# Layer 0 of a decoder trunk: six projection units on h without shift, and a completion of h in place

## The chip, the core and the metric

One core of a Trainium2 chip runs the whole program in one launch. The metric is device time in microseconds (us) of one execution. Before the change the median of three runs is 1299.08 us (1296.54 to 1302.62).

The engines: PE (matmuls), ACT (activations), DVE (vector operations), POOL (a second, slower vector engine), and SP, which issues most of the DMAs. Each works through its own queue in order and waits on semaphores of the others.

## The reference, cut to what matters

Two layers, 512 tokens, 1024 channels, float32. Each layer computes:

```python
def mixer_layer(x, c, positions, w_ada, b_ada, g_norm, w_in, ...):
    mod = jax.nn.silu(c) @ w_ada + b_ada                # (1, 3 * 1024)
    shift, scale, gate = jnp.split(mod, 3, axis=-1)
    h = rms_norm(x, g_norm) * (1.0 + scale[:, None, :]) + shift[:, None, :]
    z = h @ w_in                                         # (1, 512, N_IN)
    (fq, fk, fv, ff, fg, dq, dckv, diq, dik, diw, dg,
     sq, sk, sv, sg, merge) = jnp.split(z, points, axis=-1)
    ...                                                  # three causal mixers: y_fox, y_dsa, y_sb
    m_fox, m_dsa, m_sb = jnp.split(jax.nn.sigmoid(merge), 3, axis=-1)
    mixed = m_fox * (y_fox @ w_br_fox) + m_dsa * (y_dsa @ w_br_dsa) + m_sb * (y_sb @ w_br_sb)
    return x + gate[:, None, :] * (mixed @ w_out)
```

`c` is one vector, so `shift`, `scale` and `gate` are one number per channel, and each of the three is a product of a vector of 1024 with a matrix of 1024x1024 (4 MB of `w_ada`). Since h = n * s + shift (n the normed x, s = g_norm * (1 + scale)), a projection is h @ W = (n * s) @ W + shift @ W, and shift @ W is one number for each column of W.

## The kernel before

**Products.** h is kept channel-major in `hH`, `hL`: eight chunks `k` of 128 channels (partitions) by 512 tokens. Each float32 operand is split into a high part of reduced precision and the remainder, and each product is three matmuls (high*high, high*low, low*high; `mm3`). A weight tile is loaded into `raw` (or `qst`), its high part `wh` is made on ACT (L117), its low part `wl` on DVE (L121). A *unit* is 128 columns of `w_in` against all eight chunks: 24 matmuls of 512 columns into one PSUM bank.

**Order.** PE and SP work in the order of the code. The main stream is a generator; beside it a planner runs threads (attention heads, spills, later conditioning) by a clock of its own that counts PE time. ACT, DVE and POOL are ordered by a scheduler; a part of the first layer's opening puts DVE in the order of the code. `self.t(shape, type, tag, n)` takes the next of `n` buffers of a tag: a tile waits until the one that had the buffer before has been read. The DMA semaphores are eight in number, so that a ninth transfer waits for the first.

**The opening of layer 0 before.** `load_x` brings x, `setup` the parameters, `first_x` (L365) transposes x on PE and takes the norm's factors, `rope_tables` (L239) makes the tables of sines. `opening_first` (L872) then goes through four blocks `b` of 256 channels. For each, `ada_first` (L311) loads eight tiles of `w_ada` (256 columns of shift and of scale), and the sums are made on DVE (`ada_sum`) and, in part, as one-column matmuls on PE (`ada_mm`, L329); `ada_close` adds them. `scale_h` (L413) and `rest_h` (L420) then make `hH` and `hL` of the block's two chunks, and `step` runs products with them: the *small* columns (208 matmul columns wide, two banks), and three units, fox q, fox k and a fox gate. All eight chunks of x are written back to memory by `spill` (L395). Behind the opening the stream goes on with `diq(0)` (matmuls of 256 columns), the values, and the units of the merge gates (`gate0(m)`, L1045; columns from `O_MERGE`), of which `gate0(0)` comes after the second tile of values and `gate0(1)`, `gate0(2)` with the next pair.

## Time and profile before

| | us |
|---|---|
| median of three runs | 1299.08 (1296.54 to 1302.62) |
| the profiled execution: its own time | 1301.89 |
| its span | 1300.2 |
| mean granted clock of TensorE in it | 0.992 |
| PE busy | 1258.1 (97%) |
| DVE busy | 973.1 (75%) |
| ACT busy | 720.1 (55%) |
| first product / first matmul of `diq(0)` | 25.46 / 70.60 |

The profile is of one execution. A busy time is the time in which an engine had an instruction in work; matmuls overlap, so that their pace is read from their start times and not from the length of one. "Granted clock" is the share of full speed that TensorE was allowed. A bracket behind a timeline's row says how long the engine was idle just before and what ended it.

### The profile page before, as it was taken

What the parts mean: (1) busy time and instruction counts of PE and PEld (TensorE: products, weight loads), DVE (VectorE), ACT (ScalarE), POOL (GpSimd) and SP (SyncE); (2) the same over time, 40 slices, a digit from 0 to 9 for tenths busy, and PEclk for the clock granted to TensorE, in tenths of its full rate; (3) what the DMA queues carried; (4) which work ended last, traced back from release to release, by engine and by line L of the source; (5) the groups of instructions that cost most, each with busy time, mean ns of one, the idle gap of its engine ahead of it and who ended that gap; (6) DMA issues with size and microseconds to landing.
All of it is one profiled execution on the core that took longest, in us unless ns stands there. A gap on an engine that the chain in (4) does not pass through costs nothing.

```text
span 1300.2 us, 19627 instructions
## 1 busy us (share of the span) xinstructions
PE 1258.1 (97%) x7057; PEld 1087.3 (84%) x7057; DVE 973.1 (75%) x2059; ACT 720.1 (55%) x1415; POOL 154.0 (12%) x343
## 2 busy tenths in 40 slices
...
GB/s 285 151 163 99 82 113 113 99 88 75 114 91 89 115 88 90 113 137 94 148 122 91 106 66 97 81 67 99 81 65 98 66 98 66 98 81 106 94 100 73
DMA packets 193458, 133.33 MB, mean 103 GB/s; under 512 B 9457, under 2 KB 188225, under 8 KB 193361
## 3 DMA queue, kind: packets, MB, share of 16 engines
...
HBM read 125.74 MB, written 6.29 MB: 102 GB/s over the span
## 4 chain that ended last, share of the span: by engine, by line
PE 74%; DVE 14%; DMA 5%; issue 3%; ACT 2%; SPq 0%; POOL 0%; DVEq 0%; POOLq 0%; ACTq 0%
PE pg L65 57%; PE pt L65 8%; PE pa L65 5%; PE pt L69 4%; DMA raw<-in_w_in_dram 3%; DVE wl L121 3%; DVE fm L667 2%; DVE pr L668 1%; DVE score L614 1%; DVE ada L280 1%; DVE m L613 1%; ACT wh L117 1%; DVE pt L121 1%; DVE qst L123 1%; DMA vs<-in_x_dram 1%
## 5 line engine op out<-in xcount | busy, mean ns | idle before, releaser
L65 PE MATMUL pg<-hH,wh 128*128 128x512 f32 (+1 forms) x848 | 340.4, 401 | 0.5 <-ACT wh L117 0.5
L65 PE MATMUL pg<-hH,wl 128*128 128x512 f32 (+1 forms) x848 | 332.9, 393 | 0.8 <-DVE wl L121 0.8
L65 PE MATMUL pg<-hL,wh 128*128 128x512 f32 (+1 forms) x848 | 333.0, 393 | 0.0
L121 DVE TENSOR_TENSOR wl<-raw,wh 128x1024 fp32r<-128x1024 f32 (+1 forms) x178 | 217.8, 1224 | 89.6 <-ACT wh L117 88.9
L117 ACT ACTIVATE wh<-raw 128x1024 fp32r<-128x1024 f32 (+1 forms) x178 | 187.7, 1054 | 159.6 <-PE pg L65 79.3
L65 PEld LDWEIGHTS pg<-hH,wl 128*128 128x128 f32 x848 | 160.2, 189 | 37.7 <-DVE wl L121 1.0
L65 PEld LDWEIGHTS pg<-hL,wh 128*128 128x128 f32 x848 | 161.5, 190 | 26.6
L65 PEld LDWEIGHTS pg<-hH,wh 128*128 128x128 f32 x848 | 161.1, 190 | 26.8 <-ACT wh L117 0.7
L65 PE MATMUL pg<-wh,hH 128*128 128x256 f32 x448 | 128.7, 287 | 0.0
L65 PE MATMUL pg<-wh,hL 128*128 128x256 f32 x448 | 126.5, 282 | 0.0
L65 PE MATMUL pg<-wl,hH 128*128 128x256 f32 x448 | 125.8, 281 | 0.0
L117 ACT ACTIVATE pt<-pt 128x512 fp32r<-128x512 f32 x192 | 83.3, 434 | 74.9 <-PE pt L69 73.2
L65 PE MATMUL pg<-y,wh 128*128 128x512 f32 x384 | 121.2, 396 | 0.0
L121 DVE TENSOR_TENSOR pt<-pt,pt 128x512 fp32r<-128x512 f32 x192 | 92.9, 484 | 25.9 <-ACT pt L117 23.6
L624 ACT ACTIVATE pr<-pr,nm 128x128 f32<-128x128 f32 (+3 forms) x128 | 71.6, 560 | 67.5 <-DVE nm L623 67.0
L69 PE MATMUL pt<-ident,pr 128*128 128x128 f32 x480 | 85.9, 275 | 3.0 <-DVE pr L668 2.7
L626 ACT ACTIVATE pr<-pr,den 128x128 f32<-128x128 f32 (+3 forms) x128 | 71.1, 559 | 27.0 <-DVE den L625 26.2
L65 PEld LDWEIGHTS pg<-wh,hH 128*128 128x128 f32 x448 | 84.8, 189 | 0.7
L65 PEld LDWEIGHTS pg<-wl,hH 128*128 128x128 f32 x448 | 84.7, 189 | 0.7
L65 PEld LDWEIGHTS pg<-wh,hL 128*128 128x128 f32 x448 | 84.4, 188 | 0.0
L65 PE MATMUL pa<-pt,vs 128*128 128x512 f32 (+3 forms) x256 | 71.3, 352 | 11.6 <-DVE pt L121 10.9
L65 PEld LDWEIGHTS pg<-y,wh 128*128 128x128 f32 x384 | 70.2, 188 | 14.0
(216 smaller groups left out, 2337.4 us busy)
## 6 DMA issues: line engine op xcount, KB each, us to landing
raw<-in_w_in_dram SPq DMA_DIRECT2D x134, 512.0 KB, 3.8
raw<-in_w_ada_dram SPq DMA_DIRECT2D x32, 512.0 KB, 3.5
raw<-in_w_out_dram SPq DMA_DIRECT2D x16, 512.0 KB, 3.7
y<-in_w_ada_dram SPq DMA_DIRECT2D x24, 256.0 KB, 5.4
raw<-in_w_br_fox_dram SPq DMA_DIRECT2D x8, 512.0 KB, 3.7
raw<-in_w_br_sb_dram SPq DMA_DIRECT2D x8, 512.0 KB, 4.1
raw<-in_w_br_dsa_dram SPq DMA_DIRECT2D x8, 512.0 KB, 4.6
yf<-xd ACTq DMA_DIRECT2D x16, 256.0 KB, 2.9
```

What stands on the lines that cost most here:

```text
L65: self.nc.tensor.matmul(o, s, m, start=first, stop=last, skip_group_check=True)
L69: self.nc.tensor.transpose(o, i, self.ident[:n, :n])
L117: self.nc.scalar.activation(out, in_, AF.Copy, scale=scale)
L121: self.nc.vector.tensor_tensor(out, in_, hi.bitcast(F32), ALU.subtract)
L123: self.nc.vector.scalar_tensor_tensor(out, in_, scale, hi.bitcast(F32), ALU.mult, ALU.subtract)
L280: nc.vector.scalar_tensor_tensor(acc, v[:, j, :], self.sc[:, k:k + 1], acc, ALU.mult, ALU.add)
L613: self.pin(nc.vector.max(m8, s))
L614: nc.vector.match_replace(s, m8, s, SENT)
L624: nc.scalar.activation(p, p, AF.Exp, bias=nm, scale=-1.0, accum_out=den)
L626: nc.scalar.activation(p, p, AF.Copy, scale=den)
L667: nc.vector.tensor_tensor_scan(rev, rev, rev, 1.0, ALU.mult, ALU.bypass)
L668: nc.vector.tensor_tensor(s[:, :n - 1], s[:, :n - 1], u[:, 1:n], ALU.mult)
```

## The change

The first layer's opening is written anew as `first_layer`, with DVE in the order of the code throughout it.

- The parameters are loaded on ACT's queue, ahead of x; `c` gets its transposition first (`condition`), the rest follows (`params`).
- x is transposed at once, seven chunks into seven banks and the eighth after them, and n = x * rstd is made for each chunk (`norm`).
- Only *scale* is loaded in four quarters of 256 channels, with the columns of six units: fox q, k and gate (units 0 to 2) and the merge gates 0 to 2 (units 4, 5 and 3). `scale_sum` adds a quarter (quarter 0 on PE alone, with 16 one-column matmuls; the others on DVE, with a part on PE). `chunks(b)` makes `hH` and `hL` of n * s, without shift, splits the weights, and then puts n * s in the place of n.
- All six units run on this h, quarter by quarter.
- *Shift* is loaded meanwhile, in two halves of eight tiles of 128x512. `shift_sum` adds a half: ACT scales three tiles, POOL adds these, DVE adds five. `shift_close` takes the sum across partitions with eight one-column matmuls. `complete(k)` makes `hH` and `hL` anew in place, with shift.
- `unit_shift` multiplies the unsplit weights of the six units with shift: 48 one-column matmuls into one bank, from which a bias for each unit is taken. It enters the three gates through their Tanh, and units 0 to 2 by an Identity in place.
- The tables of rope, and a part of the spill, come behind the last quarter's `chunks`. The small columns come at the end, on the completed h, both halves after all else. `gate0` returns at once for the three gates that are done.

```diff
+    def first_layer(self, fox, posts, mod):
+        nc, xt = self.nc, self.xt
...
+        gates = O_MERGE
+        singles = (fox[0], fox[1], fox[2], gates + 256)
+        homes = (("qst", 6), ("kh", 5), ("kl", 5), ("yf", 4))
...
+        def load_scale(b):
+            scale[b] = []
+            for j in range(4):
+                v = self.t([P, 2, 256], F32, *(("pt", 4) if b == 2 else ("y", 8)))
+                src = w_ada[j * 256:(j + 1) * 256, D + b * 256:D + b * 256 + 256]
+                nc.sync.dma_start(v, src.rearrange("(k p) n -> p k n", p=P))
+                scale[b].append(v)
...
+        def load_shift(i):
+            shift[i] = []
+            for k in range(KC):
+                v = self.t([P, 512], F32, *(("pt", 4) if i == 0 and k >= 4 else ("y", 8)))
+                nc.sync.dma_start(v, w_ada[k * P:(k + 1) * P, i * 512:(i + 1) * 512])
+                shift[i].append(v)
...
+        def load_chunks(b):
+            if b % 2 == 0:
+                load_single(0, b // 2)
+            load_scale(b)
+            if b % 2 == 0:
+                load_single(1, b // 2)
+            load_gates(b)
+            if b % 2 == 0:
+                load_single(2, b // 2)
+                load_single(3, b // 2)
+        load_chunks(0)
+        load_chunks(1)
...
+        norm = lambda k: nc.vector.tensor_tensor(xn[k], xc[k], rb, ALU.mult)
+        norm(0)
+        norm(1)
+        def scale_sum(b, pe):
...
+            ops = [(scale[b][j][:, i, :], self.sc[:, 2 * j + i:2 * j + i + 1]) for j in pe for i in range(2)]
+            ops += [(acc, self.ones)] if js else []
+            for n, (v, s) in enumerate(ops):
+                for c in range(2):
+                    self.mm(pt[:, c:c + 1], v[:, c * P:(c + 1) * P], s, n + c == 0, n + 1 == len(ops))
+            c = slice(2 * b, 2 * b + 2)
+            nc.vector.tensor_tensor(mod[1][:, c], pt[:, 0:2], self.prm[:, 32 + 2 * b:34 + 2 * b], ALU.add)
+            nc.vector.scalar_tensor_tensor(mod[1][:, c], mod[1][:, c], 1.0, self.prm[:, 8 + 2 * b:10 + 2 * b], ALU.add, ALU.mult)
...
+        def chunks(b):
             ks = (2 * b, 2 * b + 1)
...
+            for k in ks:
+                nc.scalar.activation(self.hH[:, k, :], xn[k], AF.Copy, scale=mod[1][:, k:k + 1])
+            if b % 2 == 0:
+                split_single(0, b)
+            for k in ks:
+                nc.vector.scalar_tensor_tensor(self.hL[:, k, :], xn[k], mod[1][:, k:k + 1],
+                                               self.hH[:, k, :].bitcast(F32), ALU.mult, ALU.subtract)
+            if b % 2 == 0:
+                split_single(1, b)
+            split_gates(b)
+            if b % 2 == 0:
+                split_single(2, b)
+                split_single(3, b)
+            for k in ks:
+                nc.scalar.activation(xn[k], xn[k], AF.Copy, scale=mod[1][:, k:k + 1])
+        pss = {u: self.ps("g") for u in range(3)}
+        order = (0, 1, 4, 5, 2, 3)
+        def unit(u, b):
...
+            for k in (2 * b, 2 * b + 1):
+                if u < 4:
+                    w = [x[:, k, :] for x in wt[u]]
+                else:
+                    w = [x[:, k - 2 * b, (u - 4) * P:(u - 3) * P] for x in gw[b]]
+                self.mm3(ps, *w, h[0][k], h[1][k], k == 0, k == KC - 1)
...
+        def shift_sum(i):
+            v = shift[i]
+            for k in (1, 4, 7):
+                nc.scalar.activation(v[k], v[k], AF.Copy, scale=self.sc[:, k:k + 1])
+            nc.gpsimd.tensor_tensor(v[1], v[1], v[4], ALU.add)
+            nc.gpsimd.tensor_tensor(v[1], v[1], v[7], ALU.add)
+            acc = self.t([P, 512], F32, "tmp", 2)
+            for k in (0, 2, 3, 5, 6):
+                if k == 0:
+                    nc.vector.tensor_scalar(acc, v[k], self.sc[:, k:k + 1], None, ALU.mult)
+                else:
+                    nc.vector.scalar_tensor_tensor(acc, v[k], self.sc[:, k:k + 1], acc, ALU.mult, ALU.add)
+            sums[i] = [acc, v[1]]
+        def shift_close(i):
+            if i == 0:
+                self.late_ps = self.ps("a")
+            pt = self.late_ps
+            for n, acc in enumerate(sums[i]):
+                for j in range(4):
+                    self.mm(pt[:, 4 * i + j:4 * i + j + 1], acc[:, j * P:(j + 1) * P], self.ones, i + n + j == 0, n == 1)
+            c = slice(4 * i, 4 * i + 4)
+            nc.vector.tensor_tensor(mod[0][:, c], pt[:, c], self.prm[:, 24 + 4 * i:28 + 4 * i], ALU.add)
+        def complete(k):
+            nc.scalar.activation(self.hH[:, k, :], xn[k], AF.Identity, bias=mod[0][:, k:k + 1])
+            nc.vector.scalar_tensor_tensor(self.hL[:, k, :], xn[k], mod[0][:, k:k + 1],
+                                           self.hH[:, k, :].bitcast(F32), ALU.add, ALU.subtract)
+        def unit_shift(ks):
+            for k in ks:
+                for u in range(6):
+                    if u < 4:
+                        w = raws[u, k // 4][:, k % 4, :]
+                    else:
+                        w = raws["g", k // 2][:, k % 2, (u - 4) * P:(u - 3) * P]
+                    self.mm(self.late_ps[:, 8 + u:9 + u], w, mod[0][:, k:k + 1], False, k == KC - 1)
+        load_chunks(2)
+        scale_sum(0, range(4))
+        chunks(0)
+        norm(2)
+        norm(3)
+        load_chunks(3)
+        self.load_positions()
+        self.forget_bias()
+        for b in range(4):
+            for u in order[:4]:
+                unit(u, b)
             if b < 3:
...
+                scale_sum(b + 1, (3,))
+                chunks(b + 1)
+                if b == 0:
+                    for k in range(4, KC):
+                        norm(k)
+                if b == 1:
+                    load_shift(0)
+                if b == 2:
+                    self.rope_tables()
+                    shift_sum(0)
+                    load_shift(1)
+                    for k in range(3):
+                        nc.sync.dma_start(self.xd[k], xc[k])
+                    small = [self.small_raw(0, j) for j in range(2)]
             else:
...
+                shift_close(0)
+                for k in range(4):
+                    complete(k)
+                unit_shift(range(4))
+            for u in order[4:]:
+                unit(u, b)
+        shift_sum(1)
+        shift_close(1)
+        for k in range(4, KC):
+            complete(k)
+        unit_shift(range(4, KC))
+        ws = [self.split(v) for v in small]
+        bias = self.t([P, 16], F32, "bias")
+        nc.vector.tensor_copy(bias[:, 0:6], self.late_ps[:, 8:14])
+        nc.vector.tensor_scalar(bias[:, 8:14], bias[:, 0:6], 0.5, None, ALU.mult)
+        for m, u in enumerate((4, 5, 3)):
+            self.mix[m] = self.t([P, S], F32, "mix", 8)
+            nc.scalar.activation(self.mix[m], pss[u], AF.Tanh, scale=0.5, bias=bias[:, 8 + u:9 + u])
+        for u in range(3):
+            nc.scalar.activation(pss[u], pss[u], AF.Identity, bias=bias[:, u:u + 1])
+            posts[u](pss[u])
...
+        return xc, ws
...
-            self.new_h()
-            h = self.h()
-            rb = self.rows(st["r"], "t", range(NB))
-            yield from self.opening_first(xc, rb, mod, fox, h, sps, sms, post)
-            pss = [None, None, self.gate_ps]
-            self.spawn(self.small_post(l, sms), 3.0)
-            self.spawn(self.spill(xc), 10.0)
...
+            for u in range(2):
+                for kc in range(KC):
+                    yield from self.gemm_b(sps[u], ws, NSM, (2 * u, 2 * u + 1), (kc,))
+                self.small_take(sms, sps[u])
+            self.spawn(self.small_post(l, sms), 2.0)
+            self.spawn(self.spill(xc[3:], 3), 1.0)
+            self.mark(("fox", l, "pair", 0), 0.0)
+            return
...
         def gate0(m):
+            if self.mix[m]:
+                return
             self.mix[m] = self.t([P, S], F32, "mix", 8)
...
-        xc, r, self.rest_x = self.first_x(xt)
-        self.forget_bias()
-        self.rope_tables()
-        carry = {"r": r}
+        xc, carry = None, {}
...
+            self.load_params()
             self.xt = self.load_x()
             self.setup()
             self.go(self.program(out))
```

Where the instructions stand, at three places.

DVE, between the last quarter's work and the end of the opening. Before, the tables of rope (`rt`, `ropeC`, `ropeS`) stand among the sums of the first block (`fm`), ahead of the first `hL`:

```order
L280 SCALAR_TENSOR_TENSOR fm_235<-y_248,sc_129,fm_235 128x256
L268 SCALAR_TENSOR_TENSOR rt_45_213<-rt_44_212,rt_45_213 128x128
L280 SCALAR_TENSOR_TENSOR fm_235<-y_248,sc_129,fm_235 128x256
L269 TENSOR_SCALAR rt_45_213<-rt_45_213 128x128
L280 SCALAR_TENSOR_TENSOR fm_235<-y_254,sc_129,fm_235 128x256
L270 TENSOR_SCALAR rt_45_213<-rt_45_213 128x128
L280 SCALAR_TENSOR_TENSOR fm_235<-y_254,sc_129,fm_235 128x256
L272 TENSOR_SCALAR ropeS_198<-ropeS_198 128x4x32
L346 TENSOR_TENSOR mod_9_90<-pa_232,prm_125 128x2
L349 SCALAR_TENSOR_TENSOR mod_9_90<-mod_9_90,prm_125 128x2
L346 TENSOR_TENSOR mod_8_89<-pa_232,prm_125 128x2
```

After, they stand between the last quarter's `hL` (above these rows) and the sum of shift's first half (`tmp_567`; `y_423` and so on are its tiles); `mod_9_90` is shift, `wl_743` the low part of the small columns' first weights:

```order
L268 TENSOR_SCALAR rt_118_552<-rt_118_552 128x128
L270 TENSOR_SCALAR ropeS_537<-ropeS_537 128x4x32
L970 TENSOR_SCALAR tmp_567<-y_423,sc_154 128x512
L972 SCALAR_TENSOR_TENSOR tmp_567<-y_427,sc_154,tmp_567 128x512
L972 SCALAR_TENSOR_TENSOR tmp_567<-y_429,sc_154,tmp_567 128x512
L972 SCALAR_TENSOR_TENSOR tmp_567<-pt_433,sc_154,tmp_567 128x512
L972 SCALAR_TENSOR_TENSOR tmp_567<-pt_435,sc_154,tmp_567 128x512
L983 TENSOR_TENSOR mod_9_90<-pa_636,prm_150 128x4
L987 SCALAR_TENSOR_TENSOR hL_215<-vs_216,mod_9_90,hH_214 128x512 x4
L970 TENSOR_SCALAR tmp_695<-y_573,sc_154 128x512
L972 SCALAR_TENSOR_TENSOR tmp_695<-y_577,sc_154,tmp_695 128x512
L972 SCALAR_TENSOR_TENSOR tmp_695<-y_579,sc_154,tmp_695 128x512
```

The tables went from the front of the opening to a place ahead of the sum of shift.

ACT, at the end of the opening. Before, the last two `hH`, then copies of the small columns' result and the high parts of `diq(0)`'s weights (`wh_706`, `wh_712`):

```order
L418 ACTIVATE hH_225<-tm_607,mod_8_89 128x512
L418 ACTIVATE hH_225<-tm_610,mod_8_89 128x512
L469 COPY tm_648<-pt_223 128x416
L485 ACTIVATE rt_148_759,ssq_758<-tm_648 128x128
L485 ACTIVATE rt_149_761,ssq_758<-tm_648 128x128
L469 COPY tm_662<-pt_224 128x416
L117 ACTIVATE wh_706<-raw_704 128x1024
L485 ACTIVATE rt_150_763,ssq_758<-tm_662 128x128
L117 ACTIVATE wh_712<-raw_710 128x1024
```

After, the last tile of shift's second half is scaled (`y_587`), then come the first half's four `hH`, the second half's, the high parts of `diq(0)`'s weights (`wh_889`, `wh_895`), the Identity passes on the banks of units 0 to 2 (`pg_220` to `pg_222`), and a table load, right behind which the three gates' Tanh stand (`mix_753` from the bank `pt_308` first):

```order
L964 ACTIVATE y_587<-y_587,sc_154 128x512
L986 ACTIVATE hH_214<-vs_216,mod_9_90 128x512 x4
L117 ACTIVATE wh_742<-raw_592 128x832
L117 ACTIVATE wh_746<-raw_596 128x832
L986 ACTIVATE hH_214<-vs_217,mod_9_90 128x512 x4
L117 ACTIVATE wh_889<-raw_887 128x1024
L117 ACTIVATE wh_895<-raw_893 128x1024
L117 ACTIVATE pr_163_927<-y_925 128x128
L1045 ACTIVATE pg_220<-pg_220,bias_750 128x512
L1045 ACTIVATE pg_221<-pg_221,bias_750 128x512
L1045 ACTIVATE pg_222<-pg_222,bias_750 128x512
L1043 ACT_TABLE_LOAD
```

The four `hH` of the first half stand behind the scaling of the second half's last tile, and the Tanh of the gates behind the next projection's weights.

PE, at the end of the opening. Before, the last chunks of the three units (`pg_314`, `pg_326`, `pg_337`) are followed by `diq(0)` (`pt_716`):

```order
L65 MATMUL pg_337<-hH_225,wl_328 128x512
L65 MATMUL pg_337<-hH_225,wh_327 128x512
L65 MATMUL pg_337<-hL_226,wh_327 128x512
L65 MATMUL pg_337<-hH_225,wl_328 128x512
L65 MATMUL pt_716<-wh_706,hH_225 128x256
L65 MATMUL pt_716<-wl_707,hH_225 128x256
```

After, the weights' products with shift (`pa_636`) are followed by the small columns (`pt_785`); their second half, 48 rows on, goes to `pt_786`, which takes the bank of `pt_308`, the first merge gate's:

```order
L65 MATMUL pa_636<-mod_9_90,qst_288 128x1 x2
L65 MATMUL pa_636<-mod_9_90,qst_223 128x1
L65 MATMUL pa_636<-mod_9_90,kh_233 128x1
L65 MATMUL pa_636<-mod_9_90,kl_237 128x1
L65 MATMUL pa_636<-mod_9_90,yf_239 128x1
L65 MATMUL pa_636<-mod_9_90,qst_288 128x1 x2
L65 MATMUL pt_785<-wh_742,hH_214 128x208
L65 MATMUL pt_785<-wl_743,hH_214 128x208
L65 MATMUL pt_785<-wh_742,hL_215 128x208
```

What stood among the units' products before, the small columns, now stands alone between the completion and `diq(0)`.

## Rows read from the trace of the kernel before

**Rows 1.** The page's head: the span, and each engine's busy time, its share of the span and its instructions.

```profile
span 1300.2 us, 19627 instructions
...
PE 1258.1 (97%) x7057; PEld 1087.3 (84%) x7057; DVE 973.1 (75%) x2059; ACT 720.1 (55%) x1415; POOL 154.0 (12%) x343
```

**Rows 2.** The timeline of PE in 0 to 71 us: start, length of one, engine, line, operation, out<-in, tile (weights, then result), how many in a row; in brackets the idle time before and what ended it.

```profile
14.26 6.82 PE L65 MATMUL pa<-sc,y 128*128 128x1 f32 x32
...
25.46 0.54 PE L65 MATMUL pt<-wh,hH 128*128 128x208 f32 x1 [1.72 <-ACT hH L418]
...
31.93 0.41 PE L65 MATMUL pt<-wl,hH 128*128 128x208 f32 x1
32.14 0.38 PE L65 MATMUL pt<-wh,hL 128*128 128x208 f32 x1
...
40.45 3.41 PE L65 MATMUL pa<-sc,y 128*128 128x1 f32 x16
...
50.88 0.27 PE L65 MATMUL pt<-wl,hH 128*128 128x208 f32 x1
50.99 0.28 PE L65 MATMUL pt<-wh,hL 128*128 128x208 f32 x1
...
54.20 1.84 PE L65 MATMUL pa<-sc,pt 128*128 128x1 f32 x16
...
69.67 0.40 PE L65 MATMUL pg<-hH,wl 128*128 128x512 f32 x1
...
70.60 0.28 PE L65 MATMUL pt<-wh,hH 128*128 128x256 f32 x1
```

**Rows 3.** Windows of 10 us: length, then busy time (and instructions) of PE, PEld, DVE, ACT and POOL, the clock granted to PE, DMA share, GB/s.

```profile
40.00:50.00 10.00, 10.00 (x41) 9.11 (x39) 6.80 (x15) 1.38 (x2) 0.00 (x0) 0.53 0.69 223
...
80.00:90.00 10.00, 8.15 (x68) 7.65 (x67) 7.10 (x15) 5.48 (x8) 0.00 (x0) 1.00 0.76 207
90.00:100.00 10.00, 8.28 (x68) 7.88 (x66) 6.55 (x14) 7.23 (x15) 1.74 (x5) 1.00 0.20 69
100.00:110.00 10.00, 9.04 (x71) 8.88 (x72) 9.77 (x24) 7.75 (x17) 3.10 (x6) 1.00 0.36 108
110.00:120.00 10.00, 9.75 (x78) 9.34 (x77) 9.90 (x24) 7.42 (x16) 2.33 (x5) 1.00 0.54 155
```

**Rows 4.** The waits behind the opening, 80 to 102 us, as rows of three timelines: four of PE, one of ACT, one of DVE.

```profile
85.30 0.44 PE L69 MATMUL pt<-ident,rq 128*128 128x128 f32 x2 [0.17 <-DVE rq L439]
...
89.55 0.41 PE L69 MATMUL pt<-ident,rq 128*128 128x128 f32 x2 [1.68 <-DVE rq L439]
...
96.39 0.39 PE L65 MATMUL pt<-y,qst 128*128 128x256 f32 x1 [0.96 <-DVE y L121]
...
100.96 0.66 PE L69 MATMUL pt<-ident,tmp 128*128 128x128 f32 x4 [1.71 <-DVE tmp L439]
...
85.49 1.06 ACT L117 ACTIVATE wh<-raw 128x1024 fp32r<-128x1024 f32 x1 [2.63 <-DMA raw<-in_w_in_dram]
...
86.58 1.23 DVE L121 TENSOR_TENSOR wl<-raw,wh 128x1024 fp32r<-128x1024 f32 x1 [1.34 <-ACT wh L117]
```

**Rows 5.** Instructions of 0 to 70 us by line, engine, operation and shape: busy time in us, mean ns of one; then the idle time before them and what ended it.

```profile
L422 DVE SCALAR_TENSOR_TENSOR hL<-tm,mod,hH 128x512 fp32r<-128x512 f32 x8 | 5.8, 747 | 0.9 <-ACT hH L418 0.7
...
L418 ACT ACTIVATE hH<-tm,mod 128x512 fp32r<-128x512 f32 x8 | 5.5, 720 | 15.7 <-DVE tm L417 15.7
...
L121 DVE TENSOR_TENSOR wl<-raw,wh 128x1024 fp32r<-128x1024 f32 x3 | 3.7, 1224 | 0.8 <-ACT wh L117 0.8
L117 ACT ACTIVATE wh<-raw 128x1024 fp32r<-128x1024 f32 x3 | 3.2, 1055 | 0.6 <-DMA raw<-in_w_in_dram 0.6
L379 ACT COPY mix<-pt 128x512 f32<-128x512 f32 x5 | 2.8, 574 | 1.1 <-PE pt L69 1.1
...
L117 ACT ACTIVATE wh<-qst 128x512 fp32r<-128x512 f32 x4 | 2.5, 620 | 0.2 <-DMA qst<-in_w_in_dram 0.2
...
L121 DVE TENSOR_TENSOR wl<-raw,wh 128x832 fp32r<-128x832 f32 x2 | 2.0, 1020 | 0.3 <-ACT wh L117 0.3
...
L271 ACT ACT_TABLE_LOAD x1 | 1.3, 1283 | 0.0
...
L268 DVE SCALAR_TENSOR_TENSOR rt<-rt,rt 128x128 f32<-128x128 f32 x2 | 0.6, 286 | 0.0
...
L264 DVE TENSOR_SCALAR rt<-rq 128x128 f32<-128x128 f32 x2 | 0.4, 222 | 0.0
...
L271 ACT ACTIVATE ropeC<-rt 128x128 f32<-128x128 f32 x1 | 0.3, 309 | 0.2 <-DVE rt L270 0.2
L209 POOL TENSOR_SCALAR_AFFINE_SELECT pen<-pen 128x128 f32<-128x128 f32 x1 | 0.3, 297 | 0.0
```

**Rows 6.** DMA: what was moved in each of 40 slices of 0 to 60 us (1.5 us each), the total of that stretch, and from the whole page the KB of an issue and the median us from issue to landing.

```profile
GB/s 0 115 421 423 418 52 160 288 272 282 332 309 264 279 288 307 338 341 356 354 346 346 184 302 242 285 323 288 350 367 315 56 0 0 11 0 12 238 192 0
DMA packets 17605, 14.19 MB, mean 236 GB/s; under 512 B 3441, under 2 KB 17089, under 8 KB 17601
...
raw<-in_w_in_dram SPq DMA_DIRECT2D x134, 512.0 KB, 3.8
...
yf<-xd ACTq DMA_DIRECT2D x16, 256.0 KB, 2.9
```

256 lines of the change are left out of this document (93 added, 163 removed).

## The prediction

> **What bounds the kernel now.** I read the page's totals first: PE is busy 97% of the span [rows 1], so time can only come from the stretches where PE waits, or from work that it no longer does. The windows say where the first layer's opening has such stretches. PE starts its first product only at 25.46, having waited 1.72 us for ACT's hH [rows 2]; it then works without a gap to the end of the opening at 70.60, but partly at the lower of its two clock levels: the granted clock is 0.53 in 40 to 50 [rows 3], and the 208-column products start 0.21 us apart at 31.93 against 0.11 at 50.88 [rows 2]. The next idle PE stands behind the opening: 8.15 and 8.28 busy in 80 to 100, and there the weights are what is late (ACT waited 2.63 for one to land, DVE 1.34 for ACT) [rows 3, 4]. From 100 on DVE has become the full engine: 9.77 and 9.90 of 10 [rows 3].
>
> **What the change does, step by step.** It starts products earlier (only `scale` is needed for the first h) and pulls three gate units forward; it pays with a second pass over h, with one-column products for the weights' shift, and with a chain at the end that nothing covers.
>
> *Start.* The transposes of the first half of x are done by 14.26 [rows 2], as before. Then come 16 one-column products for quarter 0 of scale: 16 such took 1.84 [rows 2], so 16.1. Add a short DVE step (estimate 0.3) and one hH, 0.72 [rows 5]: products start at about 17.3 instead of 25.46, 8.2 earlier.
>
> *Quarters.* A quarter is 6 units of 2 chunks of 3 products, 36 x 0.2325 (four products from 69.67 to 70.60, [rows 2]) = 8.4, plus 0.7 for the six one-column products of the next scale (6 x 0.115). I take the first 6.7 us at the lower clock, as from 25.46 to 32.14 before [rows 2]; this costs 3.3. The four leading units of quarters 0 to 3 then end at about 26, 35, 44.5 and 54. Loads should not bound it: columns of six units are 1.5 MB more than of three, on the 14.19 MB of the first 60 us, and from 12 to 45 us most slices moved 260 to 370 GB/s, with little left to move behind 47 [rows 6].
>
> *The tail.* At 54 PE wants the sum of the first half of shift. It stands on DVE behind hL of quarter 3 (I have it end at 49.9) and behind the tables of rope, which before stood among the sums of the first block. Their price: two tables of four scalar steps (0.22), three of 0.28, one sine (0.31) and one more scalar step (0.22) [rows 5], 2 x 2.26 = 4.5, and an estimated 1.1 for the start and the hand-overs between ACT and DVE: 55.5. The first step of the sum ends at 56.1 and the other four (0.75 each, hL's price [rows 5]) at 59.1: PE waits 5. From the first step hangs a chain of buffers, because a tile of the second half of shift can only be loaded into the place that this step frees:
>
> transfer of y 2.9 (such a tile's time in [rows 6]) to 59.0; scaling on ACT 0.65 (between 0.62 and 0.72 [rows 5]) to 59.7; an add on POOL; the last tile's transfer, 2.9, which waits for that add; its scaling. No POOL add of 512 columns is in the trace: POOL took 0.30 for a select over 128 columns [rows 5], so four times that is 1.2; the bounds are 0.3 and 2.4 (twice), and I take 1.2. The last tile is scaled at 64.4. Only behind it, in ACT's order, stand the four hH of the first half (4 x 0.72 = 2.9, 67.3), and the hL follow (the last 0.75 later, 68.0); behind these on DVE the five steps of the second sum (3.5, 71.5), eight one-column products (1.7 at the lower clock's 0.213, from 3.41 for 16 [rows 2]; 0.9 at the higher), the bias (0.2), hH x 4 (2.9), the last hL (0.75), and the low part of the small weights, 1.02 [rows 5]: **78.1**. PE's own work beside it (two units, 48 one-column products) fits in the 19 us from 59.1.
>
> Then small: two halves of 48 products at 0.11 [rows 2]. The first runs at once, to 83.4. The second wants the bank that Tanh of the first gate unit frees. On ACT this Tanh stands behind two splits of the next unit's weights. Their loads wait for the small split on DVE: 78.1 + 3.8 [rows 6] + 1.06 [rows 5] = 82.9, the second split at 84.0, three Identity passes over 512 columns (0.57 each, the price of the copies from PSUM [rows 5]) after DVE has made the bias at 85.2, 86.9; a table load 1.28 [rows 5], Tanh 0.6 as such a copy: 88.8. The second half ends at 94.1, and there the next projection (128x256, at 70.60 before [rows 2]) begins.
>
> *The opening's sum.* Before, that projection begins at 70.60, with three gate units still to come later: 72 x 0.232 = 16.7, so 87.3 on the same count. After: 94.1. **Loss 6.8.** PE's sum alone would be 17.3 + 4 x 8.4 + 2.1 + 3.3 + 10.6 for small + 9 for the one-column work of the tail = 76; 18 us of the tail are waiting.
>
> *Given back.* The waits behind the opening (0.17, 1.68, 0.96 and 1.71, together 4.5 [rows 4]) come from weights that landed late. After the change these are split by 84 to 85, 9 us ahead of their use. Bounds 0 (the releaser by name is the rotation on DVE, and may stay) and 4.5; I take 3.2, since ACT's 2.63 and DVE's 1.34 of waiting there [rows 4] stand right ahead of the two larger ones.
>
> *Taken away.* The three gate units no longer fill the stretch 100 to 120, where DVE is full: 16.7 us of PE work leave, with only 3 x 1.22 of DVE work [rows 5]. PE is still 9.04 and 9.75 busy there [rows 3], and attention is paced by PE's clock in the planner, so other projections move up. Bounds 0 and 6.5 (half of 16.7 - 3.7); I take 1, near the idle time that the stretch shows now.
>
> Rests: 37 more PE instructions, the ACT and DVE passes of the completion: all inside the tail already counted. Spills and the small loads now stand behind the last shift tile on SP's queue, and land by 69, before they are wanted: nothing.
>
> **Sum.** 6.8 - 3.2 + 1.0 = +4.6 on the profiled execution's 1301.89, 1306.5. That execution was 2.8 above the median of the runs, 1299.08; on the median's scale 1303.7, +0.35%.
>
> **The rivals.** *A, slower: the filler is missed.* Nothing is given back and DVE's stretch costs 4 to 6 more, because units with posts on DVE take the gates' place: 6.8 + 4 = +11, 1310. For it: 9.77 and 9.90 [rows 3]. Against: PE's waits [rows 4] lie ahead of that stretch and begin with weights. It decides if DVE's projections in 90 to 130 stand without slack.
>
> *B, faster: the tail is hidden.* If the rope tables or the buffers cost PE little (hand-overs quicker, POOL at 0.3, the Tanh earlier), the opening ends near PE's sum plus some 6 us of waiting, 82: 5 ahead of 87.3, and with 3 given back -8: 1291. For it: the start is 8 earlier and no product is lost. Against: four steps of the chain are transfers and ACT passes whose prices the trace shows [rows 5, 6].
>
> *C, slower: the tail at the lower clock.* From 59 to 78 PE does almost nothing but one-column products and waiting. Behind such work the trace shows a granted clock of 0.53 in 40 to 50 and 0.213 per one-column product [rows 2, 3]; yet in 80 to 100, with 1.8 us idle of 10, it stayed at 1.00 [rows 3]. The first half of small at the lower clock would hide (78.1 + 10.2 = 88.3, before Tanh at 88.8); if the second also runs so, 48 x 0.10 = 4.9 more: 1308.6. The Trainium skill ("TensorE: Matmul & The Clock Gate", section "Part 1: The HAM clock gate") says that "the default state is throttled, and activity releases the throttle". By that rule this tail, with its waits, ends throttled, and the sum would be C's; the row of 40 to 50 agrees, those of 80 to 100 show waits without a fall, and none shows a tail of this length.
>
> *D, the change doesn't start early.* If quarter 1 or 2 waits for its weights (eight transfers in flight, shared with scale), the 8 us of the start go: 6 to 8 slower than the forecast, 1310.
>
> **How the numbers follow.** Forecast 0.44, A 0.22, B 0.16, C 0.12, D 0.06. About 0.5% (6.5 us) is what a measurement of this kernel can tell from no change, so the borders are 1292.6 and 1305.6. The forecast's own range, 1300 to 1307, lies within them but for 0.08 of its 0.44; of B 0.13 is below, 0.03 within; of A 0.06 within, 0.16 above; of C 0.02 within, 0.10 above; D above. Faster 0.13, same 0.47, slower 0.40. The range 1292 to 1313 leaves out most of B and the far end of A.
>
> **What would show it.** Right: first product near 17; PE idle or one-column from 54 to 78; the wait for y's transfer and Tanh as releasers there; the 128x256 projection at 94; smaller waits at the same place in the program behind. Wrong: that projection before 88 (B), or after 97 (C, D); or a like opening and a longer 100 to 140 with DVE as releaser (A).

## The result

| | before | after |
|---|---|---|
| median of the runs, us | 1298.67 (1296.54 to 1302.62) | 1316.51 (1316.05 to 1317.95) |
| ratio | | 1.0136 (95% interval 1.0110 to 1.0161) |
| profiled execution: time, span | 1301.89, 1300.2 | 1316.05, 1314.3 |
| first product / first 256-column product of `diq(0)` | 25.46 / 70.60 | 18.63 / 106.05 |

The median of the kernel before is over four executions now, and so differs from the 1299.08 given at the start. The changed kernel is 17.8 us slower by the medians (14.1 by the two profiled executions); 4.6 were forecast, and the range ended at 1313. The head of its page (against [rows 1]):

```profile
span 1314.3 us, 19829 instructions
...
PE 1265.5 (96%) x7134; PEld 1104.0 (84%) x7134; DVE 975.7 (74%) x2061; ACT 734.2 (56%) x1443; POOL 158.6 (12%) x347
```

Its PE timeline in the opening (against [rows 2]):

```profile
12.88 4.55 PE L65 MATMUL pa<-sc,y 128*128 128x1 f32 x32
18.63 0.80 PE L65 MATMUL pg<-hH,wh 128*128 128x512 f32 x1 [1.20 <-ACT hH L929]
...
57.67 0.39 PE L65 MATMUL pt<-hH,pr 128*128 128x512 f32 x1
62.41 1.16 PE L65 MATMUL pa<-ones,tmp 128*128 128x1 f32 x8 [4.35 <-DVE tmp L972]
63.43 1.85 PE L65 MATMUL pa<-ones,y 128*128 128x1 f32 x8
65.53 0.59 PE L65 MATMUL pa<-mod,qst 128*128 128x1 f32 x2 [0.25 <-DVE mod L983]
65.98 0.56 PE L65 MATMUL pa<-mod,kh 128*128 128x1 f32 x2
66.41 0.57 PE L65 MATMUL pa<-mod,kl 128*128 128x1 f32 x2
66.83 1.42 PE L65 MATMUL pa<-mod,yf 128*128 128x1 f32 x6
...
74.52 1.42 PE L65 MATMUL pa<-mod,yf 128*128 128x1 f32 x6
75.80 0.77 PE L65 MATMUL pg<-hH,wh 128*128 128x512 f32 x1
...
80.69 0.95 PE L65 MATMUL pa<-ones,tmp 128*128 128x1 f32 x8
...
82.78 0.38 PE L65 MATMUL pa<-mod,qst 128*128 128x1 f32 x2 [0.26 <-DVE mod L983]
...
91.45 0.99 PE L65 MATMUL pa<-mod,qst 128*128 128x1 f32 x4
92.30 0.52 PE L65 MATMUL pt<-wh,hH 128*128 128x208 f32 x1
...
100.60 0.36 PE L65 MATMUL pt<-wh,hH 128*128 128x208 f32 x1 [0.34 <-ACT mix L1043]
...
106.05 0.29 PE L65 MATMUL pt<-wh,hH 128*128 128x256 f32 x1
```

Read the counts: a `shift_close` of eight one-column products stands as two rows of x8, that is 16 PE instructions, and one chunk's six products with shift as 12. **Each float32 one-column product is two PE instructions.** From 65.53 to 75.80 PE does the first 24 of them, from 82.78 to 92.30 the second 24, 0.20 to 0.21 us per instruction. From 62.41 until the small columns begin at 92.30 PE has no wait longer than 0.26. The forecast's wait for DVE ahead of that is there (4.35 at 62.41, forecast 5). The windows of the same stretch (columns as in [rows 3]) show the clock that went with it:

```profile
60.00:70.00 10.00, 7.34 (x37) 7.28 (x38) 3.38 (x5) 3.11 (x5) 2.54 (x2) 0.66 0.71 220
70.00:80.00 10.00, 10.00 (x38) 9.13 (x39) 5.62 (x9) 2.58 (x4) 0.00 (x0) 0.50 0.24 50
80.00:90.00 10.00, 9.74 (x57) 9.47 (x56) 4.77 (x7) 2.56 (x4) 0.00 (x0) 0.67 0.17 52
90.00:100.00 10.00, 10.00 (x60) 10.00 (x60) 2.80 (x5) 5.56 (x8) 0.00 (x0) 0.64 0.86 249
```

0.50, the lower level, in all of 70 to 80, and 0.64 to 0.67 around it. ACT's timeline shows the chain of Tanh that the forecast had found: two transfers, two splits, Identity, a table load.

```profile
67.61 0.72 ACT L964 ACTIVATE y<-y,sc 128x512 f32<-128x512 f32 x1 [4.62 <-DMA y<-in_w_ada_dram]
...
82.76 2.56 ACT L986 ACTIVATE hH<-vs,mod 128x512 fp32r<-128x512 f32 x4 [8.77 <-DVE mod L983]
90.69 1.06 ACT L117 ACTIVATE wh<-raw 128x1024 fp32r<-128x1024 f32 x1 [5.36 <-DMA raw<-in_w_in_dram]
94.30 1.06 ACT L117 ACTIVATE wh<-raw 128x1024 fp32r<-128x1024 f32 x1 [2.56 <-DMA raw<-in_w_in_dram]
...
98.56 1.28 ACT L1043 ACT_TABLE_LOAD   x1
```

Tanh follows at 99.86 and releases the second half of the small columns at 100.60; PE waited for it only 0.34, since it came late itself. The chain hangs on the close of shift's second half: the row at 82.76 waits for its `mod`, and that close stands on PE behind the first 24 products.

Behind the opening the forecast gain is there. PE busy in the 100 us from the 256-column projection on, after:

```profile
106.05:206.05 100.00, 98.75 (x655) 90.42 (x654) 83.34 (x189) 69.19 (x142) 22.03 (x39) 1.00 0.33 96
```

and before, in the same place of the program (the waits of [rows 4] among them):

```profile
70.60:170.60 100.00, 95.22 (x629) 86.53 (x628) 82.01 (x184) 69.23 (x133) 19.83 (x37) 1.00 0.42 122
```

4.78 us idle before, 1.25 after. Much of the rest of the span's gain behind the projection is not waits but the pace of the products; "The pitch" below is on that.

### The profile page after: what moved, and what is told of

Same layout as the page of the kernel before. It is cut to its first block, busy times and chain, and to the rows that moved or that the text cites. A ratio compares the mean times of both kernels' runs of the same rounds, so it can differ in the third digit from the quotient of the medians.

```text
span 1314.3 us, 19829 instructions
## 1 busy us (share of the span) xinstructions
PE 1265.5 (96%) x7134; PEld 1104.0 (84%) x7134; DVE 975.7 (74%) x2061; ACT 734.2 (56%) x1443; POOL 158.6 (12%) x347
## 4 chain that ended last, share of the span: by engine, by line
PE 60%; DVE 20%; DMA 9%; ACT 5%; issue 4%; POOL 0%; ACTq 0%; DVEq 0%; SPq 0%; POOLq 0%
PE pg L65 46%; PE pt L65 8%; DMA raw<-in_w_in_dram 5%; DVE wl L121 4%; PE pa L65 4%; PE pt L69 3%; ACT wh L117 2%; DVE fm L595 2%; DVE ada L278 2%; DVE m L541 1%; DVE pt L121 1%; DVE score L542 1%; DVE pr L596 1%; DMA yf<-in_w_in_dram 1%; DVE qst L123 1%
## 5 line engine op out<-in xcount | busy, mean ns | idle before, releaser
L65 PE MATMUL pg<-hH,wh 128*128 128x512 f32 (+1 forms) x824 | 329.4, 400 | 2.3 <-ACT hH L929 1.2
L65 PE MATMUL pg<-hH,wl 128*128 128x512 f32 (+1 forms) x824 | 321.3, 390 | 0.8 <-DVE wl L121 0.8
L65 PE MATMUL pg<-hL,wh 128*128 128x512 f32 (+1 forms) x824 | 321.0, 390 | 0.0
L121 DVE TENSOR_TENSOR wl<-raw,wh 128x1024 fp32r<-128x1024 f32 (+1 forms) x174 | 212.4, 1222 | 101.7 <-ACT wh L117 100.9
L117 ACT ACTIVATE wh<-raw 128x1024 fp32r<-128x1024 f32 (+1 forms) x174 | 183.4, 1054 | 156.5 <-PE pg L65 81.4
L65 PEld LDWEIGHTS pg<-hH,wl 128*128 128x128 f32 x824 | 156.4, 190 | 34.5 <-DVE wl L121 1.0
L65 PEld LDWEIGHTS pg<-hH,wh 128*128 128x128 f32 x824 | 156.9, 190 | 26.7 <-ACT wh L117 1.3
L65 PEld LDWEIGHTS pg<-hL,wh 128*128 128x128 f32 x824 | 157.0, 191 | 25.2 <-DVE hL L933 0.9
L552 ACT ACTIVATE pr<-pr,nm 128x128 f32<-128x128 f32 (+3 forms) x128 | 71.5, 558 | 61.8 <-DVE nm L551 61.0
```

Of the source, the lines that this page charges most:

```text
L65: self.nc.tensor.matmul(o, s, m, start=first, stop=last, skip_group_check=True)
L117: self.nc.scalar.activation(out, in_, AF.Copy, scale=scale)
L121: self.nc.vector.tensor_tensor(out, in_, hi.bitcast(F32), ALU.subtract)
L552: nc.scalar.activation(p, p, AF.Exp, bias=nm, scale=-1.0, accum_out=den)
```

## The experiments

Theory 1: PE's own one-column products bind the tail. Theory 2, the prediction's: the chain of buffers, scaling, POOL and transfers does. Theory 3: the lower clock is the loss. Theory 4: the three gates were worth keeping as filler. Theories 5 to 7 are on the pitch, at the end (5: the places of the tiles in SBUF set it; 6: the chip or the day; 7: the place of `wh`, by itself in 7a, against the others in 7b). Where no diff names another base, the base is the changed kernel. "Projection" is the first 256-column product.

**e1, a quarter of the products with shift.**

```diff
-            for k in ks:
+            for k in ks[:1]:
                 for u in range(6):
```

> This kernel leaves out 36 of the 48 one-column products of the weights with shift (chunks 0 and 4 alone are done), so the bias of the six units is incomplete. Theory 1 (these products, two PE instructions each, 96 in all at 0.214 us, are what the tail waits for): the second sum on DVE, ready at 75.8 before, takes over, the 256-column projection starts at 96 to 98 instead of 106.05, and the time falls by 8 to 10, to about 1307. Theory 2 (the chain of buffers, ACT scaling, POOL add and transfers sets the end of the tail, as the prediction had it): 0 to 2 less, 1314 to 1316.

1308.48, ratio 1.0062 (1.0046 to 1.0079): 8.0 less than the changed kernel. 36 of the 48 products are left out. Its PE timeline:

```profile
75.77 1.76 PE L65 MATMUL pa<-ones,tmp 128*128 128x1 f32 x8 [2.20 <-DVE tmp L972]
...
79.50 0.59 PE L65 MATMUL pa<-mod,qst 128*128 128x1 f32 x2 [0.25 <-DVE mod L983]
...
82.08 0.52 PE L65 MATMUL pt<-wh,hH 128*128 128x208 f32 x1
...
97.32 0.29 PE L65 MATMUL pt<-wh,hH 128*128 128x256 f32 x1
```

The small columns begin at 82.08, 10.2 sooner: the products were the path to them. Now PE does wait for the second sum (2.20 at 75.77): the forecast's chain is the next thing behind, and not the first. The projection starts at 97.32, 8.7 sooner and inside theory 1's 96 to 98, but that number has a second cause. The scheduler gave ACT another order here, with Tanh ahead of the next projection's weights, and so PE did not wait for Tanh:

```profile
88.08 1.84 ACT L1043 ACTIVATE mix<-pt,bias 128x512 f32<-128x512 f32 x3
...
91.49 1.06 ACT L117 ACTIVATE wh<-raw 128x1024 fp32r<-128x1024 f32 x1
```

In the changed kernel's order Tanh begins 17.1 behind the row of the second `hH` (82.76 to 99.86); from e1's 79.48 that would be 96.6, and the projection would come at about 103 (an estimate from these rows). So the 10.2 is what this run shows of the products; the 8.7 is in part the other order.

**e7, the last two units ahead of the close.**

```diff
-            else:
+            for u in order[4:]:
+                unit(u, b)
+            if b == 3:
                 shift_close(0)
...
-            for u in order[4:]:
-                unit(u, b)
```

> The last two units of quarter 3 go ahead of the close of shift's first sum on PE (they need nothing of shift), where PE waited 4.35 for DVE. Theory 1 (PE's own order and count of instructions set the tail): the 12 products run at 58 inside the wait, and the 4.9 us that they took behind the weights' products at the lower clock leave the path; the 256-column projection starts at about 101 instead of 106.05, time 1310 to 1313. Theory 2 (the buffers' chain): 0. What follows the opening has differed by up to 6 us between kernels with the same instructions there, so the start of that projection is the sharper measure.

Projection at 102.78 (3.3 sooner, 5 expected); 1316.17, ratio 1.0107 (1.0085 to 1.0129). The units fit into the wait, which shrinks to 2.25; the second close then starts at 75.69. The median doesn't follow: what comes behind the projection took 1211.9 us here and 1208.25 in the changed kernel, with the same PE work. Over the runs with that work it is 1208.3 to 1214.9, so an edit's few us are read at the projection's start and not from the time. That start has a scatter of its own: in the kernel before it was 70.60 in one profile and 68.84 in another (b_same).

**e2, the sum ahead of rope.**

```diff
-                    self.rope_tables()
                     shift_sum(0)
                     load_shift(1)
+                    self.rope_tables()
```

> The tables of rope are made on DVE behind the sum of shift's first half and not ahead of it. Theory 1: PE's wait of 4.35 at 62.41 goes, all behind it comes 4 to 4.5 earlier, and rope's 5.6 us on DVE lie beside PE's one-column products; about 1312. Theory 2: the whole chain comes 5.6 earlier, 1311. A rival to both, that the tables are late for the projection that needs them or hold up the first hL with shift: no gain.

No gain: projection at 106.03, 1320.15. DVE's timeline shows why:

```profile
57.03 1.33 DVE L262 TENSOR_SCALAR rt<-rq 128x128 f32<-128x128 f32 x1
...
63.71 0.23 DVE L270 TENSOR_SCALAR ropeC<-ropeC 128x128 f32<-128x128 f32 x1 [3.59 <-ACT ropeC L269]
...
66.36 0.15 DVE L983 TENSOR_TENSOR mod<-pa,prm 128x4 f32<-128x4 f32 x1
```

The sum is done at 57, but `mod`, shift itself, stands behind rope in DVE's order, and rope's first table waited 3.59 for ACT. PE waited 7.62 for `mod`. What is moved behind a sum must also go behind the use of its result; e8 does that.

**e8, both, with rope last.** e7's edit, and:

```diff
-                    self.rope_tables()
                     shift_sum(0)
...
         ws = [self.split(v) for v in small]
+        self.rope_tables()
```

> The changed kernel with the last two units of quarter 3 ahead of the close of shift's first sum, and the tables of rope behind the small columns' weights, last of the opening on DVE. Nothing is left out. Theory 1: PE's waits of 4.35 and the 4.9 of the two units leave the tail; the 256-column projection starts at 96 to 99 instead of 106.05 (102.78 with the first of the two edits alone), time 1306 to 1311. Theory 2 (the chain of Tanh and of the next weights' loads holds the second half of the small columns): not under 101.

Projection at 99.89 (6.2 sooner), 1314.35, ratio 1.0125 (1.0102 to 1.0149): a little later than theory 1 had it and sooner than theory 2's 101; 1.09 of it is a wait for Tanh at 94.44. Tidying the order brings back a third of the opening's loss. PE now goes from quarter 3 into the one-column products without the wait, and waits nowhere longer than 0.25 until 90; the granted clock falls all the same:

```profile
63.20:90.50 27.30, 27.05 (x127) 26.96 (x127) 17.79 (x38) 9.83 (x15) 0.27 (x1) 0.50 0.46 124
```

**e4, the sum on DVE alone.**

```diff
-            for k in (1, 4, 7):
-                nc.scalar.activation(v[k], v[k], AF.Copy, scale=self.sc[:, k:k + 1])
-            nc.gpsimd.tensor_tensor(v[1], v[1], v[4], ALU.add)
-            nc.gpsimd.tensor_tensor(v[1], v[1], v[7], ALU.add)
-            for k in (0, 2, 3, 5, 6):
+            for k in range(KC):
...
-            sums[i] = [acc, v[1]]
+            sums[i] = [acc]
```

> The two sums of shift are made on DVE alone (eight steps each); no scaling on ACT, no add on POOL, so the last tile's transfer doesn't wait for an add, and the first half's hH don't stand behind its scaling. Theory 1: the first sum, for which PE waits, becomes 2.3 longer (three steps of 0.77), PE has four one-column products (8 instructions) fewer in each sum, -0.9 to -1.7; the second sum stays hidden: 0 to 2 more than the changed kernel, 1316 to 1319. Theory 2: the chain becomes 3 to 4 shorter, 1312 to 1314.

1319.8, ratio 1.0147 (1.0086 to 1.0208). The time is just above theory 1's range, but the projection, at 102.99, comes 3.1 sooner, as much as theory 2 has the chain shorter. PE's rows don't show a chain, though: behind the first sum it has no wait longer than 0.40. The first sum itself comes at 62.20, as before: it takes 2.4 longer, but in this execution quarter 3's leading units ended at 55.7 instead of 58.1, because the clock did not fall at 50, and PE waits 6.54. Then PE has eight instructions fewer in each close, starts the second set at 81.30, and does it in 8.0 instead of 9.5, with more of it at the higher clock. With that much luck of the clock in it, this run does not tell the theories apart.

**e3, one-column products between wide ones**, in the last two units of quarter 3:

```diff
+                        self.mm(pss[u], s, m, False, n == 2 and k == 7)
+                        next(beside, None)       # beside = unit_shift(range(4)), now a generator
+                        next(beside, None)
...
```

> The first 24 one-column products of the weights with shift are put between the 12 products of 512 columns of the last two units of quarter 3, two behind each, instead of ahead of them. Nothing is left out. Theory 3 (the loss is the lower clock, which PE falls to because it does nothing but one-column products): the clock stays at its higher level in 66 to 80, the pitch of the one-column instructions falls from 0.214 to 0.115 and that of the 512-column ones from 0.43 to 0.23, 5 to 7 less, 1310. Theory 1 in its plain form (the count of instructions, at the clock of a tail that has long waited): 0 to 2 less.

Slower: projection at 108.50, 1324.8. The window of 70 to 80:

```profile
70.00:80.00 10.00, 10.00 (x41) 9.30 (x40) 5.69 (x9) 2.65 (x4) 0.00 (x0) 0.50 0.26 54
```

The clock stays at 0.50: the 12 wide products and the 48 instructions take 15.4 us together (66.04 to 81.40), which is 0.43 and 0.214 each, as one after the other in the changed kernel. Mixing in this proportion doesn't lift it.

**e6, 64 equal columns instead of one.**

```diff
-self.mm(self.late_ps[:, 8 + u:9 + u], w, mod[0][:, k:k + 1], False, k == KC - 1)
+self.mm(self.late_ps[:, 64 * u + 64:64 * u + 128], w, mod[0][:, k:k + 1].to_broadcast([P, 64]), False, k == KC - 1)
...
```

> The weights' products with shift get a moving operand of 64 equal columns instead of one; the result is the same. Theory 3 (PE's tail is slow because its clock falls to the lower level under one-column products): the granted clock is 1.00 in 64 to 92, the instructions start 0.115 apart instead of 0.214, and the second sum on DVE (ready at 75.8) takes over; the 256-column projection starts at 96 to 99, time 1306 to 1310. If the clock stays at the lower level: no gain, or up to 2 more.

1321.86, ratio 1.0152 (1.0127 to 1.0177). The first set stays at the lower clock (67.07 to 77.15, 0.214 each, 0.51 in 70 to 80). The second set now runs at full clock (window 80 to 90, and the rows from 83.42 to 88.80: 5.4 for 48 instructions, 0.112 each, against 9.5):

```profile
83.42 0.44 PE L65 MATMUL pa<-mod,qst 128*128 128x64 f32 x2 [0.25 <-DVE mod L983]
...
88.80 0.34 PE L65 MATMUL pt<-wh,hH 128*128 128x208 f32 x1
...
100.94 0.54 PE L65 MATMUL pt<-wh,hH 128*128 128x208 f32 x1 [6.55 <-ACT mix L1043]
...
109.31 0.30 PE L65 MATMUL pt<-wh,hH 128*128 128x256 f32 x1
```

```profile
80.00:90.00 10.00, 9.75 (x82) 9.40 (x81) 4.77 (x7) 2.56 (x4) 0.00 (x0) 1.00 0.10 23
90.00:100.00 10.00, 4.39 (x40) 4.21 (x38) 2.80 (x5) 5.23 (x7) 0.00 (x0) 0.84 0.91 264
100.00:110.00 10.00, 9.06 (x54) 9.06 (x55) 4.78 (x8) 8.69 (x19) 0.00 (x0) 0.65 0.19 70
```

The 4 us won are lost again: PE waits 6.55 for Tanh, and the second half of the small columns then runs at the lower clock (0.65 in 100 to 110, projection at 109.31). The chain of Tanh hangs on the second close, which the second set cannot move (`hH` at 83.39 here, 82.76 in the changed kernel), and so it ends at the same time to within 0.4 us. Theory 3 has its effect (rival C's mechanism, at rival C's place), but a quicker second set alone gains nothing. What a quicker first set would gain, ahead of that close, no run shows.

**e5, three units; the gates stay.** No gate columns are loaded, split or given to Tanh.

```diff
-        singles = (fox[0], fox[1], fox[2], gates + 256)
+        singles = (fox[0], fox[1], fox[2])
...
-        order = (0, 1, 4, 5, 2, 3)
+        order = (0, 1, 2)
...
-                for u in range(6):
+                for u in range(3):
...
```

> Only fox q, k and gate run on h without shift; the three merge gates stay where they were before the change. Theory 1: 24 instead of 48 products with shift (10.3 us less of PE's tail) and no Tanh in front of the small columns; the opening ends at 80 to 86, which with the three gates' 16.7 behind it stands against 106.05: 3 to 9 less, 1308 to 1313. Theory 4 (the change loses by taking three gate units from the stretch where DVE is full): far less, 1298 to 1302. Both theories leave it slower than before, whose opening ended at 70.60, unless theory 4 holds.

Projection at 90.55, 1310.42, ratio 1.0074 (1.0046 to 1.0101). Later than theory 1's 86; with the gates' 16.7 it stands at 107.25 on the changed kernel's count, and yet the whole is 6 quicker. The gates are cheaper where they were.

**e10, three units, tidied.** It adds e8's two edits to it:

> The same two edits on the version with three units (merge gates in their old place). Theory 1: the 256-column projection starts at 84 to 87 instead of 90.55, time 1303 to 1307; the chain of buffers now binds PE between the two sums, so not all of the 4.85 of waiting comes off. If the gates' place as filler, and the faster pitch of the products, are what held this version at 1310, it comes within 0.5% of the kernel before, without passing it.

Projection at 84.13, 1305.93, ratio 1.0068 (1.0042 to 1.0095). Start and time are as expected; 0.7% behind the kernel before is a little more than the 0.5% expected. With no gates moved, the completion at the end costs more than the earlier start brings.

**e9, the gates twice.**

```diff
         def gate0(m):
-            if self.mix[m]:
-                return
```

> The changed kernel, but the three merge gates are computed once more at their old place (the first results are not used). Theory 1: PE has hardly a wait behind the opening that they could fill (98.75 busy of the 100 us from the 256-column projection on), so the whole 3 x 24 products come on top: +15 to +17 on the changed kernel, 1331 to 1334. Theory 4 (the gates were filler): +4 to +10, 1320 to 1327, with the later stretches' waits shorter.

1324.88, ratio 1.0182 (1.0160 to 1.0204): 6 (by the ratios) to 8.8 (by the spans) for 16.7 us of PE work. Theory 4. From the projection to the end PE was idle for 35.9 us in the changed kernel and for 30.3 in e9:

```profile
106.05:1314.32 1208.27, 1172.36 (x6662) 1020.21 (x6660) 919.16 (x1950) 684.49 (x1362) 149.03 (x298) 0.99 0.32 95
```

```profile
107.35:1323.07 1215.72, 1185.42 (x6734) 1031.73 (x6732) 927.23 (x1953) 689.97 (x1368) 150.90 (x298) 1.00 0.33 95
```

So 5.6 us of the gates' work went into waits. The other few us that it didn't cost are no more than this stretch varies by with the same work. Two windows of 100 us, 200 us behind the projection, of the changed kernel:

```profile
306.05:406.05 100.00, 93.37 (x508) 79.46 (x507) 96.81 (x188) 48.30 (x95) 17.97 (x43) 1.00 0.30 92
406.05:506.05 100.00, 93.59 (x547) 81.19 (x547) 75.64 (x170) 56.09 (x117) 9.08 (x17) 0.98 0.30 90
```

and of e9 at the same distance behind its projection:

```profile
307.35:407.35 100.00, 95.94 (x507) 81.57 (x506) 94.10 (x182) 49.12 (x96) 19.52 (x43) 0.98 0.33 95
407.35:507.35 100.00, 95.70 (x532) 81.78 (x530) 80.66 (x168) 57.64 (x120) 13.54 (x23) 1.00 0.35 101
```

13.0 us of PE idle against 8.4: most of the waits that the gates filled lie here, and not in 100 to 120: the stream has run ahead by three units.

**The pitch.** In comparing the traces behind the opening, e9 and e5 took 13 to 14 us less there than the kernel before with the same instructions and nearly the same idle time of PE (30.3 and 30.6 against 32.7). The difference is the pitch: over some 2900 places in each trace where one 512-column product starts 0.20 to 0.28 us behind another, the mean is 0.2331 before and 0.2290 after. The next runs ask where that is from; no instruction changes in them, only unused first tiles, which move where tiles lie in SBUF (b_wh, b_pad and a_pad are below; the others take a first tile of up to twelve tags, and b_layout, b_h and a_old_places allocate h early):

```diff
         mod = {part: self.t([P, 8], F32, f"mod{part}", 2) for part in (0, 1)}
+        self.t([P, 1024], F32R, "wh", 4)          # b_wh
+        self.t([P, 32], F32, "pad")               # b_pad, a_pad
```

> The kernel before, unchanged, profiled on the chip of the experiments. In its first profile the products of 512 columns start 0.2334 us apart through the whole program, in the changed kernel and all its variants 0.2290 to 0.2300; 3368 such products behind the opening make 13 us of that. Theory 5 (the program, by where its tiles lie in SBUF, sets the pitch): 0.233 again, time as before. Theory 6 (the chip or the day): 0.229, and the time would fall with it.

> The kernel before, with unused first tiles allocated in nearly the order in which the changed kernel allocates (weights' low parts at 40256 instead of 131136, hH at 138560 instead of 65600 bytes); no instruction is added. Theory 5: the pitch of the 512-column products falls from 0.2334 to about 0.2295, 11 to 13 us less, 1286 to 1289. Theory 6, or another property than these places: no change, 1296 to 1303.

> The changed kernel with unused first tiles allocated so that the large tiles lie nearly where the kernel before has them (hH at 56640, weights' high parts at 23872, low parts at 122176 bytes); no instruction is added. Theory 5 (the change got a faster pitch of products from where its tiles happen to lie): the pitch of the 512-column products rises from 0.2295 to 0.233, 8 to 12 us more than the changed kernel, 1324 to 1329. If it stays, the pitch hangs on other tiles than these: 1314 to 1319.

> The kernel before, with only the weights' low parts moved, to 40256 bytes right behind the high parts (hH then at 81984). Theory 5a (the low parts beside the high parts set the pitch): 0.2295, 1287 to 1293. Theory 5b (the place of hH and hL, which in all quick kernels lie above 131072 bytes and the weights below): 0.233, 1296 to 1303.

> The kernel before, with hH moved to 105792 and hL to 122176 bytes and the low parts at 163904, far from the high parts. Theory 5a: 0.233, 1296 to 1303. Theory 5b: hH is still below 131072 and most of hL above it, so products with hL alone are quicker, 1294 to 1300; if all are quick, the distance of hH from the weights' high parts decides.

> The kernel before, with one unused first tile that puts the weights' high parts at 23872 bytes instead of 24000; two tiles of 128 bytes in all go behind them, everything else keeps its place. Theory 7 (the place of the high parts sets the pitch; it is what all the quick kernels share): 0.2295, 1288 to 1294. If large tiles or something else do: 0.233, 1296 to 1303.

> The kernel before with a tile of 128 bytes in front, so that nearly all tiles lie 128 bytes later (high parts 24128, low parts 131264, hH 65728; the distances among them as before). Theory 7a (the high parts' own place: 24000 leaves 192 over a multiple of 256, the quick 23872 and 24128 leave 64): 0.2295, 1288 to 1294. Theory 7b (their place against hH and the low parts, 128 apart within 256 in the kernel before and 0 in all the quick ones): 0.233, 1296 to 1303.

> The changed kernel with the same tile of 128 bytes in front: high parts at 24000 as in the kernel before, hH at 139200, distances among them unchanged. Theory 7a: 0.233, 8 to 12 more than the changed kernel, 1324 to 1329. Theory 7b: 0.2295, 1314 to 1319.

| run | `wh` | `wl` | `hH` | `wh` to `hH`, within 256 | pitch, us | time, ratio to before |
|---|---|---|---|---|---|---|
| b_same | 24000 | 131136 | 65600 | 128 | 0.2331 | 1300.91, 1.0005 (0.9985 to 1.0025) |
| b_pad | 24128 | 131264 | 65728 | 128 | 0.2331 | 1299.77, 0.9996 (0.9982 to 1.0009) |
| b_wh | 23872 | 131136 | 65600 | 0 | 0.2292 | 1295.12, 0.9953 (0.9930 to 0.9976) |
| b_wl | 23872 | 40256 | 81984 | 0 | 0.2291 | 1291.82, 0.9952 (0.9926 to 0.9978) |
| b_h | 23872 | 163904 | 105792 | 0 | 0.2291 | 1294.01, 0.9957 (0.9933 to 0.9980) |
| b_layout | 23872 | 40256 | 138560 | 0 | 0.2291 | 1290.98, 0.9951 (0.9930 to 0.9973) |
| changed kernel | 23872 | 40256 | 139072 | 0 | 0.2290 | 1316.51, 1.0136 |
| a_old_places | 23872 | 122176 | 56640 | 0 | 0.2290 | 1321.60, 1.0176 (1.0141 to 1.0211) |
| a_pad | 24000 | 40384 | 139200 | 0 | 0.2292 | 1320.76, 1.0151 (1.0135 to 1.0166) |

Two rows each of PE's timeline, the ends of a run of 512-column products: 11 starts apart in b_same, 2.57 / 11 = 0.2336,

```profile
1003.53 0.40 PE L65 MATMUL pg<-hH,wh 128*128 128x512 f32 x1
...
1006.10 0.39 PE L65 MATMUL pg<-hH,wl 128*128 128x512 f32 x1
```

and 14 apart in b_wh, 3.20 / 14 = 0.2286:

```profile
1000.61 0.39 PE L65 MATMUL pg<-hH,wh 128*128 128x512 f32 x1
...
1003.81 0.39 PE L65 MATMUL pg<-hH,wl 128*128 128x512 f32 x1
```

Theory 6 (chip or day) falls with b_same. Theory 5 in its first form falls with a_old_places, b_wl and b_h: far moves of `hH` and `wl` keep the quick pitch. b_wh moves `wh` by 128 bytes, with two tiles of 128 bytes, and has it. 7a falls with b_pad and a_pad: `wh` may itself lie at 24000. What is left is 7b: slow where `wh` lies 128 off the others within 256, quick where it doesn't. Which of the others is the partner was not tried, and it is not simply a product that reads `wh`: the products of `hH` with `wl` changed as much (0.2331 before, 0.2291 in b_h). b_wh, the kernel before with one unused tile, and b_layout are quicker than both kernels. The pitch came in every run as 7b has it, the time did not follow in full: b_layout, b_wl, b_h and b_wh are 6 us quicker by their ratios (2.6 to 9.6 by the intervals) and 8.5 to 15 by the profiled spans, where 3368 products at the lower pitch would make 13 (an estimate from the two pitches). That is left open.

## Why the prediction was wrong

| step | predicted | measured |
|---|---|---|
| first product | 17.3 | 18.63 |
| leading units of quarter 3 end | 54 | 57.9 |
| PE's wait for the first sum | 5 | 4.35 |
| small columns begin | 78.1 | 92.30 |
| projection begins | 94.1 | 106.05 |
| opening against 87.3 | +6.8 | +18.8 |
| waits behind the opening | -3.2 | -3.5 |
| gates no longer filler | +1 | +5.6 (by idle time) to +11 (by time) |
| pitch of products | not there | -6 |
| sum | +4.6 | +17.8 |

The last two terms are read from times, or from one pair of traces, in a stretch that varies by some 6 us with the same work; so the column adds up to 15 to 20, and the sum is no closer than that.

**The step that failed is "PE's own work beside it (two units, 48 one-column products) fits in the 19 us".** It priced a product by the rows of [rows 2] as if x16 were 16 products; they were 8, as the program's 16 products at the start (x32, 4.55 us, in the rows above) show. The x32 at 14.26 in [rows 2] was such a sum of 16, too, and the head of the page has 77 more PE instructions (7134 against 7057) where the prediction wrote 37. Counted rightly, 48 products are 96 instructions, 20.5 us at 0.214, plus the two closes and the two units at 0.43; beside a 19 us chain they do not fit, they are the path. The prediction had PE waiting for 18 us of the tail; it waited 5.2 (4.35, 0.25, 0.26 and 0.34). e1 shows it: with three quarters of the products out, the small columns begin at 82.08, only 4.0 behind the forecast, which is what the quarters were late (3.9). The order listing counts products and the profile instructions, and the forecast multiplied one by the price of the other.

The lower clock has a part in this that was not measured by itself. At e6's 0.112 the 96 instructions would be 10.8 us (an estimate), and that would have fitted; it takes the count and the clock together. The prediction had both prices, 0.115 and 0.213.

The same error is in the start: its sum took 4.55 where 1.84 was forecast, of which 1.4 came back because it could begin at 12.88 instead of 14.26; the products are 1.3 late. And it is in the quarters: they are 2.6 longer than worked out beyond the late start, 2.0 of it since their one-column products took 4.1 instead of 2.1 (x8 and x4 for six products, three times), the rest by waits of 0.20 and 0.68 for DVE. What the clock cost the quarters was near the forecast (3.5, in two falls, against 3.3). Two sums of the prediction are a little off by themselves: 14.26, 1.84, 0.3 and 0.72 make 17.1, and the leading units end at 53.4 by its own prices, not 54.

**Right:** the 4 to 5 us wait for DVE's sum behind rope; the Tanh chain (e6 shows it binding at 100.9); the waits behind the opening, given back to within 0.3. The buffers' chain was right too (the last tile scaled at 67.61 + 0.72, forecast 64.4, and the second sum made at 75.8, forecast 71.5, about as late as the quarters; a POOL add, taken at 1.2, took 1.27); it was simply not the longest.

**Mis-sized:** the gates as filler. The 1 was taken from the idle time of 100 to 120. By idle time the gates filled 5.6, within the bounds of 0 to 6.5; by time it is 16.7 less 6 to 8.8, above them. The waits lay where the stream stood later (DVE 96.81 of 100 in 306 to 406), and not only where the units had stood.

**Not seen at all:** the pitch. In the forecast it could not be: it takes the second trace. The kernel before gains 6 (ratios 0.9951 to 0.9957) when it gets such places, so the change's loss without that luck would be some 6 larger than the two times show. That is measured on the kernel before, and not shown for the changed one: a_old_places and a_pad, which were to give the changed kernel the slow pitch, kept the quick one and came 4 to 5 later at their medians, within what the stretch behind the opening varies; why is open.

**Rivals.** A's second half (the filler) happened beside the forecast's own miss. C's clock happened (0.50 in 70 to 80), on the one-column products and the first half of the small columns (0.213 apart up to 97.3) rather than on their second half, and e6 shows that lifting it for the second set alone gains nothing. The Trainium skill's sentence quoted with C ("TensorE: Matmul & The Clock Gate", section "Part 1: The HAM clock gate") names activity as what releases the lower clock; the trace of e6 agrees, where the wait of 6.55 was followed by 0.65. It does not foretell e8, where PE was busy for 27.05 of 27.30 us and ran at 0.50 under one-column products and the first small columns. B and D did not happen.
